# Moving one subtraction behind the sums that TensorE waits for, and reordering the rest of VectorE's and ScalarE's work around it

## The chip, the cores and the metric

One core of a Trainium2 chip. The metric is device time in microseconds (us) of the whole program, and lower is better. TensorE (PE in the profile) multiplies, VectorE (DVE) and ScalarE (ACT) do elementwise work, GpSimd (POOL) and SyncE (SP) start transfers. PEld is TensorE's loading of weights.

## The reference, cut to what matters

```python
m, k, n = 2048, 2048, 2048
x = np.matmul(a, b)
rms = np.sqrt(np.mean(x ** 2, axis=-1, keepdims=True) + eps)
return (gamma * x / rms).astype(np.float32)
```

## The kernel before: the parts that matter

The kernel cuts the 16 row blocks into groups of two and makes each group's product with seven block products in place of eight (the additions and subtractions of quarters of A and B that this needs are made beforehand, on VectorE). `a_sums(g, (5, 2, 1))` makes such sums of A's quarters, each 128x1024 of fp16. A product is eight matmuls over K into one PSUM bank.

Rows 0 to 3 are the head; for rows 2 and 3 the right half (called the pair) is made from seven products too. Its end overlaps with the start of the first regular group, G0, which holds blocks 4 (HB) and 5. This is the seam that the change edits:

```python
    p6 = new_bank()
    product(PAIR, 1, 6, p6)
    a_sums(G0, (5,))                          # needs block HB, which ScalarE copied
    nc.vector.tensor_tensor(out=x22, in0=pair[1], in1=x22, op=ALU.subtract)
    for g in range(2):
        turn(HB + 1, g)                       # TensorE transposes block HB + 1
        take_transposed(HB + 1, g, turned[HB + 1, g], nc.vector.tensor_copy)
    square_half(0, 1)
    square_half(1, 1)
    take_rms(0)                               # a tiny reduction, then a root on ScalarE
    a_sums(G0, (2, 1))                        # sum 2 needs block HB + 1
```

The group's half then runs product 5, 2, 1, 4, 3, 7, 6, with other work hooked in between (hook n stands after the n-th product):

```python
        at_hook(0)
        p2, p5 = new_bank(), new_bank()
        one, two = ((5, p5), (2, p2)) if first else ((2, p2), (5, p5))
        product(g, j, *one)
        nc.scalar.copy(out=c, in_=one[1])
        last_squares()
        at_hook(1)
        product(g, j, *two)                   # in the first half: the product of sum 2
        nc.vector.tensor_tensor(out=t, in0=two[1], in1=c, op=ALU.add)
        at_hook(2)
        p1 = new_bank()
        product(g, j, 1, p1)
        ...
```

## Time and profile before

| | kernel before |
|---|---|
| median of the first 3 executions | 221.98 us (221.81 to 222.76) |
| span of the profiled execution | 219.9 us |
| TensorE busy | 95% |
| start of sum 2's product / natural start | 69.32 / 68.69 us |

The page of the kernel before, parts 1 and 4 (busy time by engine; shares of the span in the chain of work that ended last):

```profile
PE 209.3 (95%) x1032; PEld 97.4 (44%) x1032; DVE 165.9 (75%) x326; ACT 127.0 (58%) x263; POOL 36.3 (16%) x75
...
PE 65%; DMA 23%; ACT 4%; POOL 2%; issue 1%; DVE 1%; ACTq 0%; POOLq 0%
```

TensorE is 95% busy but holds only 65% of the chain. The rest of the chain is loads (DMA) and a short stretch of ScalarE and VectorE ahead of 69.32; the prediction shows that stretch line by line. "Natural start" is used all through: the start of sum 5's product plus eight matmuls of 0.2157 us, which is when the next product could begin if nothing held it.

### The profile page before, as it was taken

To read this page: it belongs to the slowest core of one execution; us is meant where nothing else is said; L and a number is where in the kernel's file an instruction comes from. 1 tells how busy PE (TensorE), PEld (TensorE's weight loads), DVE (VectorE), ACT (ScalarE), POOL (GpSimd) and SP (SyncE) were. 2 spreads that over 40 slices of the span, in tenths; PEclk is the share of its full clock that TensorE was granted. 3 is DMA by queue.
4 is the path that set the end of the run, shared out by engine and by line. 5 is a ranking of instruction groups with operands and counts; after the bars stand their busy time and mean duration, and the time that the engine had idled before them with its cause. 6 is when DMAs were issued, how large, how long until landed. Compare 5 with 4: busy or idle time off the path is not lost.

```text
span 219.9 us, 3044 instructions
## 1 busy us (share of the span) xinstructions
PE 209.3 (95%) x1032; PEld 97.4 (44%) x1032; DVE 165.9 (75%) x326; ACT 127.0 (58%) x263; POOL 36.3 (16%) x75
## 2 busy tenths in 40 slices
PE   7799999999999999999999999999999999999970
PEld 3344544444454444444444444444444444444440
DVE  1128799999889999979795639946695659787781
ACT  2110002920599898688745997289747996334471
POOL 7544443343020002100200002000200000000040
PEclk9999999999999999999999999999999999999996
DMA  7999999999929895948799049965699249145045
GB/s 157 164 203 206 199 206 208 212 206 228 409 76 362 291 293 118 358 176 230 213 300 405 3 93 265 351 247 95 156 294 405 42 100 364 73 174 210 1 171 212
DMA packets 36864, 46.60 MB, mean 212 GB/s; under 512 B 22256, under 2 KB 26352, under 8 KB 35568
## 3 DMA queue, kind: packets, MB, share of 16 engines
q0 software_dynamic: 10608, 23.86, 44.1%
q1 hardware_dynamic: 25824, 22.02, 33.5%
q10 hardware_dynamic: 416, 0.52, 0.7%
q8 instruction: 8, 0.13, 0.2%
q14 instruction: 8, 0.07, 0.1%
HBM read 34.60 MB, written 16.78 MB: 234 GB/s over the span
## 4 chain that ended last, share of the span: by engine, by line
PE 65%; DMA 23%; ACT 4%; POOL 2%; issue 1%; DVE 1%; ACTq 0%; POOLq 0%
PE acc L285 64%; DMA b<-in_b_dram 14%; DMA early<-in_a_dram 5%; DMA a<-in_a_dram 4%; ACT sq L219 2%; POOL b L102 1%; ACT at_even L192 1%; PE acc L790 1%; POOL early L106 1%; DVE s L260 1%; DVE at_even L192 0%; ACT x L729 0%; DVE x L551 0%; ACT norm L222 0%; ACT x L531 0%
## 5 line engine op out<-in xcount | busy, mean ns | idle before, releaser
L285 PE MATMUL acc<-b,s 128*128 128x512 bf16 x408 | 93.3, 379 | 0.5 <-DVE s L260 0.5
L285 PEld LDWEIGHTS <-s 128*128 128x128 f16 (+1 forms) x512 | 49.9, 98 | 60.4 <-DVE s L260 1.0
L388 PE MATMUL acc<-b,head_at 128*128 128x512 bf16 x176 | 43.2, 379 | 1.2 <-DMA b<-in_b_dram 1.2
L303 ACT ACTIVATE sq<-x 128x512 bf16<-128x512 f32 x53 | 33.4, 630 | 6.9 <-DVE x L722 3.0
L370 DVE SCALAR_TENSOR_TENSOR x<-x,r,gamma_sb 128x1024 f32<-128x1024 f32 x28 | 34.8, 1282 | 0.7
L219 ACT ACTIVATE sq<-a 128x1024 bf16<-128x1024 f32 x24 | 25.3, 1053 | 2.1 <-DMA a<-in_a_dram 1.5
L388 PEld LDWEIGHTS <-head_at 128*128 128x128 bf16 x176 | 16.9, 98 | 20.6 <-issue 1.6
L242 ACT ACTIVATE head_at<-a,s 128x2048 f16<-128x2048 f32 x10 | 20.0, 1998 | 3.3 <-DVE s L229 3.3
L102 POOL DMA_DIRECT2D b<-in_b_dram x32 | 17.2, 540 | 20.8 <-DMA b<-in_b_dram 15.0
L430 ACT COPY x<-acc 128x512 f32<-128x512 f32 x5 | 2.9, 582 | 24.7 <-PE acc L388 24.7
L285 PEld LDWEIGHTS <-head_at 128*128 128x128 f16 (+1 forms) x112 | 10.9, 98 | 13.2
L285 PE MATMUL acc<-early,head_at 128*128 128x512 bf16 x64 | 14.5, 379 | 0.0
L285 PEld LDWEIGHTS <-at_even 128*128 128x128 f16 x96 | 9.4, 98 | 11.3
L285 PE MATMUL acc<-early,s 128*128 128x512 bf16 x56 | 14.2, 379 | 0.0
L260 DVE TENSOR_TENSOR s<-head_at 128x1024 f16<-128x1024 f16 (+5 forms) x22 | 13.4, 635 | 0.1
L609 DVE TENSOR_TENSOR x<-x,x 128x512 f32<-128x512 f32 x9 | 6.2, 692 | 8.8 <-ACT x L607 8.3
L127 POOL COPY pace<-x 128x1 f32<-128x1 f32 x4 | 1.7, 413 | 66.7 <-DVE x L618 65.6
L591 ACT COPY x<-acc 128x512 f32<-128x512 f32 x9 | 5.2, 573 | 11.5 <-PE acc L285 11.5
L173 DVE COPY head_at<-tbank 128x1024 bf16<-128x1024 bf16 x7 | 4.8, 692 | 8.7 <-PE tbank L168 8.5
L285 PE MATMUL acc<-t_left,s 128*128 128x512 bf16 x48 | 11.3, 379 | 0.0
L774 POOL TENSOR_SCALAR x<-x,r 128x512 f32<-128x512 f32 x1 | 2.7, 2652 | 51.2 <-DVE r L346 51.2
L276 DVE TENSOR_TENSOR b<-b 128x1024 bf16<-128x1024 bf16 x16 | 10.8, 684 | 0.2
(113 smaller groups left out, 237.5 us busy)
## 6 DMA issues: line engine op xcount, KB each, us to landing
out_dram<-x SPq DMA_DIRECT2D x29, 512.0 KB, 3.8
a<-in_a_dram POOLq DMA_DIRECT2D x10, 1024.0 KB, 8.7
b<-in_b_dram POOLq DMA_DIRECT2D x32, 256.0 KB, 10.0
a<-in_a_dram POOLq DMA_DIRECT2D x4, 512.0 KB, 9.8
early<-in_a_dram POOLq DMA_DIRECT2D x7, 256.0 KB, 10.2
gamma_sb<-in_gamma_dram POOLq DMA_DIRECT2D x2, 512.0 KB, 8.3
out_dram<-x SPq DMA_DIRECT2D x3, 256.0 KB, 2.6
out_dram<-a SPq DMA_DIRECT2D x1, 512.0 KB, 3.3
```

The lines of the kernel that those rows point to most:

```text
L102: nc.gpsimd.dma_start(out=raw[j][kp][:, t, :], in_=b[lo:lo + P, j * HALF:(j + 1) * HALF])
L173: nc.vector.tensor_copy(out=head_at[:, 2 * kp:2 * kp + 2, :, :], in_=view)
L219: nc.scalar.activation(out=junk, in_=a32[mb][:, h * HALF:(h + 1) * HALF], func=ACTF.Square, scale=2.0 ** -8, accum_out=n2[:, h:h + 1])
L242: nc.scalar.activation(out=a16[mb], in_=a32.pop(mb), func=ACTF.Copy, scale=factor.pop(mb))
L260: nc.vector.tensor_tensor(out=sum_of(g, s)[:, lo:hi, :], in0=x[:, lo:hi, :], in1=y[:, lo:hi, :], op=op)
L276: nc.vector.tensor_tensor(out=flat[:, 1:3, :], in0=flat[:, 1:3, :], in1=flat[:, 0::3, :], op=ALU.add)
L285: nc.tensor.matmul(bank, lhsT[:, kp, :], rhs, start=(start and kp == 0), stop=(kp == KP - 1), skip_group_check=not start)
L303: nc.scalar.activation(out=sq[:, 0:CH], in_=src, func=ACTF.Square, scale=inv_sqrt_n, accum_out=msq[mb][:, c:c + 1])
L370: nc.vector.scalar_tensor_tensor(out=x, in0=x, scalar=inverse_of[mb], in1=gamma_sb[:, h * HALF:(h + 1) * HALF], op0=ALU.mult, op1=ALU.mult)
L388: nc.tensor.matmul(bank, head_at[:, kt, r, :], head_rhs(c, kt), start=(kt == 0), stop=(kt == KT - 1))
L591: nc.scalar.copy(out=c, in_=one[1])
L609: nc.vector.tensor_tensor(out=t, in0=t, in1=x12, op=ALU.add)
```

## The change

The intent: the subtraction does not feed TensorE, so let it run behind A's sums, which do. Then the pair's rows 2 and 3 are finished ahead of the scaling of rows 0 and 1, and a square of row 2 goes to where ScalarE would wait. The diff, cut:

```diff
     a_sums(G0, (5,))
-    nc.vector.tensor_tensor(out=x22, in0=pair[1], in1=x22, op=ALU.subtract)
     for g in range(2):
         ...
     square_half(1, 1)
+    a_sums(G0, (2,))
     take_rms(0)
-    a_sums(G0, (2, 1))
+    a_sums(G0, (1,))
+
+    def pair_sub():
+        nc.vector.tensor_tensor(out=x22, in0=pair[1], in1=x22, op=ALU.subtract)
 ...
                 hook(1, take_rms, 1)
+                hook(2, pair_sub)
                 hook(2, row_factor, nxt)
-                hook(2, finish, 0, (0,))
                 hook(2, apply, nxt)
                 hook(2, row_norm, nxt + 1)
+                hook(2, pair_sums)
                 hook(2, a_sums, g, (7, 6))
-                hook(2, finish, 1, (1, 0))
+                hook(2, finish, 0, (0,))
+                hook(2, finish, 1, (1,))
                 hook(2, row_factor, nxt + 1)
-                hook(2, pair_sums)
                 hook(2, pair_ends)
+                hook(2, scale, 1, (0,))
                 hook(4, apply, nxt + 1)
-                hook(7, square_half, r2, 1)
+                hook(4, store, 1, (0,))
+                hook(7, late.insert, 0, (r2, None))
```

(`last_squares` now also takes an entry that stands for half a row.) Below, **part 1** is the subtraction and the order of sums 2 and 1, **part 2** the order of the rows, **part 3** the later square.

More of the change, by code (lines that the diff above doesn't have):

```diff
@@ L573, in last_squares @@
         while late:
-            square(*late.pop(0))
+            mb, x = late.pop(0)
+            if x is None:
+                square_half(mb, 1)
+            else:
+                square(mb, x)
     def group_half(g, j, hooks):
```

## The prediction

> **What bounds the kernel now.** I read the page first, then the chain of work that ended last, then TensorE's waits, then the timelines of the engines around the one place that stood out. The page gives PE 95% of a 219.9 us span, DVE 75%, ACT 58%, and puts PE at 65% of the chain. The chain, in order of time, shows where PE takes over for good (start, length, what):
>
> ```profile
> 66.05 0.69 DVE s L260
> 66.74 0.60 DVE x L551
> 67.34 0.27 DVE at_even L192
> 67.61 0.25 issue
> 67.86 0.68 DVE at_even L192
> 68.54 0.06 DVE tot L335
> 68.60 0.67 DVE s L260
> 69.27 0.05 issue
> 69.32 141.76 PE acc L285 x656
> ```
>
> The reader is to see two things. From 69.32 on there is one unbroken run of 656 matmuls, 141.76 us long: nothing that VectorE or ScalarE does after that is on the path, up to the last 9 us. And just before it the path runs through VectorE, item by item through the very stretch that the change edits: A's sum 5 (L260), the subtraction (L551), two copies of transposed A (L192), a tiny reduction (L335), A's sum 2 (L260). All the waits of the matmuls in the whole kernel are these (us in total, times, longest):
>
> ```profile
> PE acc L147 <- DVE pace L137: 1.4, 1, 1.4
> PE acc L388 <- DMA b<-in_b_dram: 1.2, 2, 0.7
> PE acc L285 <- DVE s L260: 0.5, 1, 0.5
> PE tbank L419 <- DVE head_at L173: 0.3, 1, 0.3
> ```
>
> Three belong to the start, which the change leaves alone. The third is the one that it can remove. TensorE's timeline gives its true size:
>
> ```profile
> 66.97 1.89 PE L285 MATMUL acc<-b,s 128*128 128x512 bf16 x8
> 69.32 1.90 PE L285 MATMUL acc<-b,s 128*128 128x512 bf16 x8 [0.46 <-DVE s L260]
> 71.06 1.89 PE L285 MATMUL acc<-t_left,s 128*128 128x512 bf16 x8
> ```
>
> Matmuls of one product start 0.216 us apart (8 of them are 1.73 us), so the product after the one at 66.97 could have started at 66.97 + 1.73 = 68.70. It started at 69.32: **0.62 us lost**, of which the view shows 0.46 as idle, because the last matmul's modelled 0.379 us overlaps the gap.
>
> **What the Trainium skill says.** "TensorE: Matmul & The Clock Gate", section "Wait — 56ns, not 53.3ns?", gives 215.7 ns from start to start for warm matmuls of 512 columns; the trace agrees (0.216 us, granted clock 1.00 here), so PE cannot go faster in this stage, only start sooner. "Perfetto Trace Analysis", section "Tensor Engine Instruction (MATMUL, LD_WEIGHTS)", says that a matmul's end is estimated and that ScalarE and VectorE are strict FIFO. The first is why I count starts; the second is why a subtraction that nothing needs yet can hold up a sum that PE needs: the trace shows VectorE's instructions in program order, 0.60 us from start to start. "PSUM — Partial Sum Buffer", Specifications, gives 8 banks; the kernel holds one for transposes and 7 for products. A delayed read of a bank can therefore stall a product, and that has to be checked below.
>
> **The change, part by part.** *1. The subtraction leaves the path.* Removed ahead of sum 2: one 128x512 subtraction that reads PSUM, 0.60 us from start to start (66.66 to 67.26), and the tiny reduction, 0.11 us (68.46 to 68.57), which hides in the wait of sum 2 for the second copy anyway. New times on VectorE: sum 5 from 66.05. The first copy waits for the transposes, which end at 66.68, so it starts at about 66.7 and the second at 67.3. The second ends at about 67.97 (0.68 each). Sum 2 reads what it wrote and started 0.03 after its end before (68.54 to 68.57): 68.0 to 68.7 with its 0.69. PE answered 0.06 after sum 2 ended (69.26 to 69.32): 68.75. PE's natural start is 68.70, so 0.05 us, at most 0.1, of the stall stays. **Gain: 0.62 − 0.05 to 0.10 = 0.52 to 0.57 us**, at the head of an unbroken PE run, so all of it goes through to the end unless a new stall takes it.
>
> *2. Sum 1 goes behind the reduction.* It runs from about 68.75 to 69.45; its product wants it at 68.75 + 1.73 = 70.48. Not on the path.
>
> *3. Work moved in the first half of the group.* This reorders VectorE without adding to it. The same operations stand there:
>
> ```profile
> 73.97 1.29 DVE L260 TENSOR_TENSOR s<-at_even 128x1024 f16<-128x1024 f16 x2
> 75.36 2.48 DVE L370 SCALAR_TENSOR_TENSOR x<-x,r,gamma_sb 128x1024 f32<-128x1024 f32 x2
> 79.78 0.68 DVE L565 TENSOR_TENSOR x<-acc,x 128x512 f32<-128x512 f32 x1
> 80.38 0.68 DVE L566 TENSOR_TENSOR x<-acc,x 128x512 f32<-128x512 f32 x1
> ```
>
> I replayed the new order with the old spacings (0.60 for a sum, 1.20 for a 128x1024 scaling, 0.75 for a row factor's four small ones, 1.3 for the two dependent pair sums). The add of the second product comes at 70.9; the subtraction at 71.5 to 72.2; the factor to 72.8; the pair sums to 74.1; sum 7 from 74.1 to 74.8, sum 6 to 75.4; three scalings, a factor and the pair ends then fall between 75.3 and 79.9, about a microsecond sooner than at 79.78 and 80.38; one scaling to 81.0. After that VectorE is where it was before, since the sum of the work is equal. PE wants sum 7 at 68.75 + 4 x 1.73 = 75.67: 0.8 us to spare. Sum 6 has 2 us.
>
> *4. Half a row of row 2 is squared later.* ScalarE's 1.06 us square moves from before the copy of the second half's first product (81.59, copy at 82.64) to after it, where ScalarE stood waiting 0.72 us for VectorE at 83.93. This frees banks and operands sooner on ScalarE, but PE waited for neither. Worth 0 to the end time.
>
> Sum: **−0.55 us**, so 221.98 − 0.55 = **221.4 us**.
>
> **The rivals.** *A: the held bank.* The subtraction is what frees the bank of the pair's product 1, and it now comes 4.8 us later (72.2 for 67.3). Were that the bank of the group's third product, wanted at 70.5, PE would stall 1.7 us and the time would be about 223.1. Against it: the bank numbers of the program before give the third product the bank that ScalarE frees at 66.5, and the pair's bank to the fourth new one, product 7. That one is wanted at 75.7, 3.4 us after the subtraction. With the assignment following the order of release, it should stay with product 7 or go to product 6.
>
> *B: the stores move behind a transpose.* Row 0's first half is now scaled by 76.6, after the queue of SyncE has begun a transpose:
>
> ```profile
> 74.67 3.18 SPq L195 DMA_TRANSPOSE head_at<-head_at  x1
> 77.91 1.05 SPq L376 DMA_DIRECT2D out_dram<-x  x2
> ```
>
> So that store is issued at about 77.9 in place of 74.1 and, with the page's 3.8 us to landing, its buffer is free near 81 to 82. ScalarE's copy of product 3 writes that buffer and ran at 80.23; row 1's half that the next half's first copy overwrites lands just after. ScalarE may thus wait 0.5 to 1.5 us. PE needs that first copy done before product 4 of the second half, at 68.75 + 9 x 1.73 = 84.3; I put its end at 83.0. A microsecond more delay than I reckon would start to cost; half a microsecond of the gain lost would give 221.9.
>
> *C: more than the stall is gained.* Excluded by the unbroken run: no other wait is there to take.
>
> *D: the gain is lost near the end,* where the last 9 us hang on stores and ScalarE. They follow PE's last matmuls, so they move with them.
>
> **Range and chances.** The gain is 0.5 to 0.6 us if neither A nor B bites, which I hold for about 85%. The three times before spread from 221.81 to 222.76, and a median of a few runs can be off by 0.2 to 0.4. That gives 221.0 to 222.1 for 8 in 10, with the upper part for B. Two per cent are 4.4 us, ten times the largest wait that the change can touch and more than twice rival A: within 2% 0.98, faster 0.01, slower 0.01.
>
> **What would show it.** Right: TensorE's waits list no entry, or one below 0.1 us, for the sums of A at L260; the gap from the product at 66.97 to the next is 1.73 to 1.85 us in place of 2.35; the unbroken run starts some 0.55 us sooner and no new wait stands in it; the pair ends run about a microsecond sooner; ScalarE's 0.72 us wait shrinks. Wrong: a PE wait on the subtraction (A), on ScalarE's copies in the second half (B), or sum 2 coming later than 68.8 because the copies of the transposed blocks wait longer for PE than I assume.

## The result, and the profile after

The changed kernel took 221.14 us (median of 6, 221.01 to 221.74); the kernel before, in the same rounds, 222.0 us. The ratio is 0.9962, interval 0.9941 to 0.9982: within 2%.

The page of the changed kernel, the same two parts:

```profile
PE 209.2 (95%) x1032; PEld 97.5 (44%) x1032; DVE 166.0 (76%) x326; ACT 126.9 (58%) x263; POOL 36.4 (17%) x75
...
PE 92%; DMA 3%; issue 1%; ACT 1%; POOL 1%; DVE 0%; ACTq 0%; POOLq 0%
```

No engine does less work. What differs in these two pages is the chain: TensorE's share is 65% before and 92% after. Most of that rise is not the change's: three later traces of the old order have 86 to 87%, and one of the new order (part 1 alone, again) has 68%, since a chain that meets a load follows the loads from there back. What the change took out of the chain is the short stretch of ScalarE and VectorE ahead of sum 2: it stands in the chain of all four traces of the old order, and in neither trace of the changed kernel. All waits of the changed kernel's matmuls (us in total, times, longest):

```profile
PE acc L147 <- DVE pace L137: 1.4, 1, 1.4
PE acc L388 <- DMA b<-in_b_dram: 1.0, 1, 1.0
PE tbank L419 <- DVE head_at L173: 0.4, 1, 0.4
```

The wait on L260 (A's sums) has left the list. That alone proves little: three later traces of the old order do not list it either, though TensorE lost 0.27 to 0.31 us there. The starts of the matmuls decide. TensorE's timeline of the changed kernel over the seam, and VectorE's:

```profile
66.88 3.73 PE L285 MATMUL acc<-b,s 128*128 128x512 bf16 x16
70.44 1.89 PE L285 MATMUL acc<-t_left,s 128*128 128x512 bf16 x8
```

```profile
65.77 0.69 DVE L260 TENSOR_TENSOR s<-at_even 128x1024 f16<-128x1024 f16 x1 [0.20 <-ACT at_even L192]
66.63 0.69 DVE L192 COPY at_even<-tbank 128x1024 f16<-128x1024 f16 x1 [0.17 <-PE tbank L185]
67.24 0.68 DVE L192 COPY at_even<-acc 128x1024 f16<-128x1024 f16 x1
67.96 0.69 DVE L260 TENSOR_TENSOR s<-at_even 128x1024 f16<-128x1024 f16 x1
```

The products of sums 5 and 2 are now merged into one entry of 16 matmuls. Sixteen unhindered ones take 3.62 us in this view and these took 3.73, so 0.1 us of stall is left. Sum 2 runs from 67.96 to 68.65, TensorE starts on it at 68.705, and its natural start was 68.606. VectorE now waits for TensorE here (0.17 us for the transposes) and not the other way round.

### The profile page after: what moved, and what is told of

Read it like the earlier page. It is cut to its first block, busy times and chain, and to the rows that moved or that the text cites. A ratio compares the mean times of both kernels' runs of the same rounds, so it can differ in the third digit from the quotient of the medians.

```text
span 219.3 us, 3043 instructions
## 1 busy us (share of the span) xinstructions
PE 209.2 (95%) x1032; PEld 97.5 (44%) x1032; DVE 166.0 (76%) x326; ACT 126.9 (58%) x263; POOL 36.4 (17%) x75
## 4 chain that ended last, share of the span: by engine, by line
PE 92%; DMA 3%; issue 1%; ACT 1%; POOL 1%; DVE 0%; ACTq 0%; POOLq 0%
PE acc L285 71%; PE acc L388 16%; DMA early<-in_a_dram 3%; PE tbank L419 2%; PE tbank L168 2%; PE acc L800 1%; POOL b L102 0%; PE tbank L185 0%; PE acc L185 0%; ACT x L739 0%; DVE head_at L173 0%; ACT sq L803 0%; ACT rms L352 0%; POOL t_left masks.py:199 0%; POOL t_left masks.py:197 0%
## 5 line engine op out<-in xcount | busy, mean ns | idle before, releaser
L219 ACT ACTIVATE sq<-a 128x1024 bf16<-128x1024 f32 x24 | 25.3, 1053 | 2.2 <-DMA a<-in_a_dram 1.6
L260 DVE TENSOR_TENSOR s<-head_at 128x1024 f16<-128x1024 f16 (+5 forms) x22 | 13.4, 636 | 0.1
```

The costliest lines, as they stand in the source:

```text
L219: nc.scalar.activation(out=junk, in_=a32[mb][:, h * HALF:(h + 1) * HALF], func=ACTF.Square, scale=2.0 ** -8, accum_out=n2[:, h:h + 1])
L260: nc.vector.tensor_tensor(out=sum_of(g, s)[:, lo:hi, :], in0=x[:, lo:hi, :], in1=y[:, lo:hi, :], op=op)
```

## The experiments

**How each trace was read.** In every trace the span is a sum of three: the start of sum 2's product, the time from there to the start of the last matmul, and a tail. The table has all of them, in us. "Copy" is the end of ScalarE's second copy of transposed block HB, which releases sum 5. The last column is the start of the product less that copy.

| kernel | copy | natural start | start | stall | to last matmul | tail | start − copy |
|---|---|---|---|---|---|---|---|
| before | 66.02 | 68.69 | 69.32 | 0.63 | 143.23 | 7.36 | 3.30 |
| before, again | 65.30 | 68.33 | 68.61 | 0.27 | 143.23 | 7.32 | 3.31 |
| without part 1 | 66.00 | 69.00 | 69.30 | 0.30 | 143.23 | 7.36 | 3.31 |
| without part 1, again | 65.73 | 68.73 | 69.04 | 0.31 | 143.24 | 7.34 | 3.31 |
| changed | 65.74 | 68.61 | 68.71 | 0.10 | 143.24 | 7.34 | 2.97 |
| changed, again | 68.61 | 71.65 | 71.75 | 0.10 | 143.23 | 7.29 | 3.14 |
| part 1 alone | 66.35 | 68.99 | 69.09 | 0.10 | 143.23 | 7.91 | 2.74 |
| part 1 alone, again | 66.46 | 69.09 | 69.19 | 0.10 | 143.23 | 7.34 | 2.74 |
| square undone | 65.56 | 68.48 | 68.58 | 0.10 | 143.23 | 7.29 | 3.02 |
| held bank | 65.77 | 68.72 | 68.82 | 0.10 | 144.84 | 7.31 | 3.05 |
| delay on the path | 65.54 | 68.35 | 70.70 | 2.35 | 144.92 | 7.33 | 5.16 |
| delay beside | 65.72 | 68.75 | 68.85 | 0.10 | 143.48 | 7.32 | 3.13 |
| sum 2 in halves | 66.96 | 69.59 | 69.59 | 0.00 | 143.46 | 7.30 | 2.64 |

Two laws stand in it. In the old order the product starts 3.3 us after the copy, in four traces of four; TensorE was ready before that in all four. In the new order it starts 0.10 us after TensorE's natural start, in seven traces of seven that kept the seam as it is. Apart from the three kernels that put in work or a held bank, and a wait of 0.23 us in the last trace, everything else is the 143.23 us that none of the reorderings touched, and starts and tails that differ from execution to execution.

### The changed kernel again

> The changed kernel once more, beside the others on the same chip. Theory (the gain is the PE stall ahead of A's sum 2, 0.53 us by the starts of the matmuls in the two traces): 0.5 us under the kernel before, ratio 0.9976. Rival (the moved work and the square help too, so that the 0.86 us between the medians is real): 0.8 to 0.9 us under it, ratio 0.996. In the profile: 1.82 us from the start of the last product but one of A's sum 5 to the product of sum 2, as in the first trace.

221.3 us, the kernel before 222.14 in the same rounds, ratio 0.9977 (0.9937 to 1.0016). The profile happened to catch a poor start: TensorE waited 2.7 us for a load of B in the head, where it had waited 1.0 us in the first trace. For the next 3.4 us TensorE was then granted half of its full clock, and everything came 3 us later (a line of the view of busy time in stretches, explained at the delay on the path below; 0.50 is the granted clock):

```profile
8.82:12.23 3.41, 3.39 (x9) 1.15 (x9) 0.00 (x0) 0.00 (x0) 1.84 (x5) 0.50 1.23 203
```

The stall ahead of sum 2 was 0.10 us all the same. The times do not part theory from rival: the ratio is the theory's, but the medians lie 0.84 us apart, as the rival said. The structure of the trace fits the theory.

### Part 1 alone, twice

```diff
 (the kernel before)
+    the subtraction removed from the seam, sum 2 ahead of take_rms(0), sum 1 behind it
+                hook(2, pair_sub)
                 hook(2, row_factor, nxt)
                 hook(2, finish, 0, (0,))
```

> The kernel before with only the subtraction moved to the start of the later stretch, and sum 2 ahead of the tiny reduction; rows 0 to 3 in the old order, the square in its old place. Theory: the whole gain, 0.5 us under the kernel before and within 0.2 us of the changed kernel; PE's wait for sum 2 is 0.1 us or gone, and no new PE wait later. Rival (the other parts carry a share): 0.2 us or more slower than the changed kernel.

222.03 us, the kernel before 222.14, ratio 0.9996 (0.9969 to 1.0023): by the times a miss for the theory. By the trace it has the short stall (0.10) and no new wait, but a late start and the one long tail of 7.91. So it ran again:

> Part 1 alone, a second time, since its times (222.03) came out like those of the kernel before although its trace has the short gap. Theory (part 1 is the cause; its first trace had late loads by chance, product at 69.10, and a long tail, 7.91): a product near 68.7 to 69.1, 0.1 us of PE stall, and a median 0.3 to 0.6 us under the kernel before. Rival (parts 2 and 3 carry the gain in time, by the tail or by the start): 222.0 again, with a tail of 7.9 again.

221.18 us, the kernel before 221.43 in these rounds, ratio 0.999 (0.997 to 1.001). The stall was 0.10 again and the tail 7.34. The rival's repeated long tail did not come: the 0.57 us by which the first trace's tail was longer belonged to that execution. A gain of 0.25 us between medians is what the seam can explain, but it is less than the 0.3 to 0.6 us expected, and the interval of the ratio includes none. Part 1 also moves the tiny reduction behind sum 2. The two steps were not run apart, but the traces part them: sum 2 starts 0.03 us after the end of the second copy in the old order (68.54, 68.57) and in the changed kernel (67.92, 67.96), so the reduction held nothing up and the subtraction did.

### The rest without part 1, twice

```diff
 (the changed kernel)
     a_sums(G0, (5,))
+    nc.vector.tensor_tensor(out=x22, in0=pair[1], in1=x22, op=ALU.subtract)
 ...
-    a_sums(G0, (2,))
     take_rms(0)
-    a_sums(G0, (1,))
+    a_sums(G0, (2, 1))
 ...
-                hook(2, pair_sub)
```

> The changed kernel with the subtraction put back ahead of the transposed copies and sums 2 and 1 together behind the reduction; the new order of rows and the later square kept. Theory: no gain, within 0.2 us of the kernel before; the gap ahead of the product of sum 2 is 2.35 us again, 0.62 us of it lost. Rival: 0.2 to 0.4 us faster than the kernel before.

221.55 us, the kernel before 222.14, ratio 0.9988 (0.9947 to 1.0028). The stall came out at 0.30, not the 0.62 that was expected: the order of work is the old one, but TensorE was later in this execution (natural start 69.00), while the product started at 69.30 as before. That is what gave the law of the 3.3 us. The median lies 0.59 us under that of the kernel before: by the times alone the rival won this round, though the interval of the ratio includes 1. So it ran again:

> The rest without part 1, a second time, since its median (221.55) lay between the two kernels. Theory: product again at landing plus 10.2 us, a stall of 0.2 to 0.6 us, time like the kernel before within 0.3 us. Rival: 221.5 again, 0.5 us under the kernel before, with a shorter tail or an earlier start that the trace shows.

221.39 us, the kernel before 221.43, ratio 0.9997 (0.9978 to 1.0017); start − copy 3.31 again, 143.24 and 7.34. Parts 2 and 3 alone show no gain in either trace, nor in these times.

### The kernel before, again

> The kernel before, submitted as if it were a change, for a second trace of it. Reading of the six traces so far: the span is the start of sum 2's product, plus 143.23 us of unbroken matmuls (the same in all six), plus a tail of 7.3 us (once 7.9). In the old order the product starts 10.20 us after the load of the first A block has landed on its last DMA engine (59.12 and 69.32; 59.10 and 69.30), or when PE is through, whichever is later. Theory: that sum holds again (product at landing plus 10.2, 143.23, tail 7.3 or 7.9), and times like those of the kernel before. Rival: something in the 143 us differs in its slower executions, so that the trace shows another figure there.

221.45 us against 221.43, ratio 1.001 (0.9974 to 1.0046). The same kernel against itself gives an interval of 0.7%, so these rounds cannot tell a few tenths of a us; the traces can. The chain of work of this trace (start, length, what):

```profile
65.33 0.69 DVE s L260
66.02 0.60 DVE x L551
...
67.89 0.67 DVE s L260
...
68.61 141.76 PE acc L285 x656
```

It is the chain that the prediction shows, 0.7 us sooner. TensorE was sooner by only 0.36 (68.33 for 68.69), so the stall shrank from 0.63 to 0.27. ScalarE's timeline shows where the other 0.36 went, in the first trace of the kernel before and then in this one:

```profile
57.18 0.59 ACT L520 COPY x<-acc 128x512 f32<-128x512 f32 x1 [11.64 <-PE acc L285]
57.93 1.06 ACT L219 ACTIVATE sq<-a 128x1024 bf16<-128x1024 f32 x1 [0.16 <-DMA a<-in_a_dram]
```

```profile
56.82 0.59 ACT L520 COPY x<-acc 128x512 f32<-128x512 f32 x1 [11.64 <-PE acc L285]
57.30 1.06 ACT L219 ACTIVATE sq<-a 128x1024 bf16<-128x1024 f32 x1
```

In both, TensorE releases ScalarE's copy at L520, and TensorE's natural start comes 11.51 us after that copy's start. In this trace the squares of block HB (L219) followed without a wait, and ScalarE's second copy of transposed HB ended 8.48 us after the start of L520. In the first trace both squares waited for the two halves of block HB's load, which landed at 57.84 and 59.12, and it was 8.84 us. **So some 0.27 us of the stall belongs to the order of the work, as both chains start at the same work of TensorE; the other 0.36 us of the first trace is the lateness of block HB's load.** In the two traces without part 1 it is 8.51 and 8.52 us, and the stall 0.30 and 0.31. The law that was expected, 10.20 us from the landing to the product, gave 10.27 here, since the load held nothing up.

### The square in its old place

```diff
 (the changed kernel)
-                hook(7, late.insert, 0, (r2, None))
+                hook(7, square_half, r2, 1)
```

> The changed kernel with the square of row 2 back in its old place, ahead of the second half's first copy. Theory (the square's place is worth nothing): within 0.2 us of the changed kernel, 221.1 to 221.4; ScalarE waits some 0.7 us again before the late squares; no new PE wait. Rival (the square carries a share): 221.5 or more.

221.6 us, the kernel before 221.43, ratio 1.0012 (0.9982 to 1.0042). In the trace no new wait of TensorE, 143.23 us, a tail of 7.29, and the profiled execution is among the fastest of all (220.88 us). So nothing in the trace charges the square. The median of the times is on the rival's side (221.5 or more), but they spread from 220.88 to 223.07, and the interval allows up to 0.2% faster and 0.4% slower than the kernel before. ScalarE's timeline, the changed kernel first, then this one:

```profile
81.55 0.57 ACT L598 COPY x<-acc 128x512 f32<-128x512 f32 x1
82.02 1.06 ACT L310 ACTIVATE sq<-x 128x1024 bf16<-128x1024 f32 x1
...
83.89 0.63 ACT L303 ACTIVATE sq<-x 128x512 bf16<-128x512 f32 x1 [0.72 <-DVE x L620]
```

```profile
81.55 1.06 ACT L310 ACTIVATE sq<-x 128x1024 bf16<-128x1024 f32 x1
...
82.60 0.57 ACT L598 COPY x<-acc 128x512 f32<-128x512 f32 x1
83.76 0.63 ACT L303 ACTIVATE sq<-x 128x512 bf16<-128x512 f32 x1 [0.59 <-DVE x L620]
```

The copy and the square have changed places; the wait after them is not filled, since the same two pieces of work stand ahead of the same add of VectorE. Only the copy comes sooner, and TensorE did not need it.

### The held bank, forced

```diff
 (the changed kernel)
-        p1 = new_bank()
+        p1 = pair[1] if first else new_bank()
```

> The changed kernel, but the group's third product (A's sum 1) is made to take the very bank that the late subtraction reads. This is rival A of the prediction, forced. Theory (a late read of a bank costs only where the next product in that bank is already waiting): PE waits at that product until the subtraction ends at about 72.0, 1.6 us after its natural start at 70.44, and all of it goes through to the end: 1.6 us slower than the changed kernel, 1.1 slower than the kernel before. Rival (slack further on swallows part of such a stall): under 1.2 us slower than the changed kernel.

222.75 us, the kernel before 222.14 in the same rounds, ratio 1.0043 (1.0005 to 1.0081); 1.45 us over the changed kernel. The first line of TensorE's waits in this trace, and then a line of its timeline:

```profile
PE acc L285 <- DVE x L561: 1.4, 1, 1.4
```

```profile
72.17 1.89 PE L285 MATMUL acc<-t_left,s 128*128 128x512 bf16 x8 [1.45 <-DVE x L561]
```

L561 is the late subtraction. The run to the last matmul grew from 143.23 to 144.84: 1.61 us, with nothing given back. So rival A of the prediction is a real mechanism of the right size; the changed kernel escapes it only because that bank goes to the group's last product, which starts long after the subtraction. (That assignment was read from the built program; the changed kernel's traces show only that no matmul waits on L561.)

### A delay on the path, and one beside it

```diff
 (the changed kernel; gamma_sb is in place by then, and the result is not used)
+    def idle_work(n):
+        for _ in range(n):
+            nc.vector.reduce_sum(out=idle, in_=gamma_sb[:, HALF:], axis=mybir.AxisListType.X)
 (on the path)
+    idle_work(2)
     a_sums(G0, (2,))
 (beside it)
                 hook(2, scale, 1, (0,))
+                hook(2, idle_work, 1)
```

> The changed kernel with two useless VectorE reductions of 128x1024 put ahead of sum 2; each should take about 1.2 us from start to start, like a 128x1024 scaling. Theory (work ahead of sum 2 is on the path, and nothing later swallows it): the product of sum 2 starts at its natural time plus 0.1 plus 2.4, the run of matmuls after it stays 143.23 us, tail 7.3: 2.4 us slower than the changed kernel. Rival (a delay here is partly absorbed later): a run shorter than 143.23, under 2 us slower.

224.19 us (223.31 to 225.39), the kernel before 221.61, ratio 1.0098 (1.0046 to 1.0149). The two reductions took 2.4 us from start to start; the stall was 2.35 where 2.5 was expected. But the run after it did not stay at 143.23: it grew to 144.92. The view of busy time in stretches (us, PE, PEld, DVE, ACT, POOL busy with counts, granted clock, DMA share, GB/s) shows why:

```profile
66.00:68.00 2.00, 2.00 (x22) 1.29 (x19) 1.89 (x4) 1.97 (x4) 0.00 (x0) 1.00 0.85 344
71.00:74.60 3.60, 3.60 (x11) 1.25 (x10) 2.30 (x5) 3.00 (x7) 0.00 (x0) 0.53 0.67 275
74.60:80.00 5.40, 5.40 (x27) 2.45 (x26) 5.22 (x13) 4.16 (x5) 0.00 (x0) 1.00 0.22 54
```

After the stall TensorE was granted 0.53 of its clock for 3.6 us: matmuls started 0.427 us apart from 71.16 to 74.15, against 0.216 before and after. So this wait was paid a second time, by 144.92 − 143.23 = 1.69 us. Neither theory nor rival had that; the delay was not absorbed, it was amplified. The held bank's 1.6 us stall was followed by no such stretch. The times of this kernel lie 2.1 us apart, so not every execution need have had it. The mean granted clocks fit that, 0.989 and 0.983 at 224.72 and 225.39 us and 0.996 at 223.66 and 223.31, but only the first was traced. The poor start of the changed kernel's second trace shows the same pair, a wait of 2.7 us and then 3.4 us at half the clock.

> The changed kernel with one such reduction, 1.2 us of VectorE, put behind the last scaling of the moved stretch. Theory (that stretch is beside the path with a known slack): the add of the second half's second product then ends 1.2 us later, at about 86.25 on the clock of the first changed trace. Product 3 accumulates into the bank that it reads and starts at 85.98, so PE waits there 0.2 to 0.4 us, and nowhere else: 0.2 to 0.4 us slower, not 1.2. Rival (VectorE is as good as the bound here): 1.2 us slower.

221.41 us, the kernel before 221.61, ratio 0.9996 (0.9949 to 1.0044). VectorE's timeline and TensorE's:

```profile
81.08 1.21 DVE L142 TENSOR_REDUCE idle<-gamma_sb 128x1 f32<-128x1024 f32 x1
...
85.65 0.68 DVE L608 TENSOR_TENSOR x<-acc,x 128x512 f32<-128x512 f32 x1
```

```profile
84.40 3.87 PE L291 MATMUL acc<-early,at_even 128*128 128x512 bf16 x16
```

The reduction pushed the add at L608 to 85.65 to 86.33, and TensorE's 16 matmuls of products 4 and 3 took 3.87 us in place of 3.62: 0.25 us of wait in the place that was named, and 143.48 in the table. Of 1.2 us added to VectorE, 0.25 reached the end. VectorE at 76% is close to the bound in this stretch, with some 0.9 us to spare, but it is not the bound.

### Sum 2 in two halves

```diff
 (the changed kernel)
-    a_sums(G0, (2,))
+    a_sums(G0, (2,), 0, KP // 2)
+    a_sums(G0, (2,), KP // 2, KP)
```

> The changed kernel with sum 2 made in two halves, so that the first four matmuls of its product can start on the first. Theory (the 0.10 us that PE still waits in every trace of the new order is the sum's own 0.69 us): the first half takes 0.4 us, PE starts at its natural time, stall 0.0 to 0.02, so 0.1 us under the changed kernel, too little for the times to show; the second half costs VectorE some 0.15 us beside the path. Rival (the matmuls wait for the whole tile all the same): a stall of 0.2 us.

221.13 us, the kernel before 221.61, ratio 0.9966 (0.9933 to 0.9999). The stall is gone to the last hundredth: TensorE's timeline has the clean 3.62 us for the 16 matmuls.

```profile
67.87 3.62 PE L285 MATMUL acc<-b,s 128*128 128x512 bf16 x16
```

This is the best seam of all, worth 0.10 us over the changed kernel by the trace, and in the fastest of its executions the lowest time seen (220.59 us). The times can't show 0.10 us. Its trace had one thing more, a 0.23 us wait at 109.3 before the second half's product 4 of the next group. There ScalarE's copy ended at 109.49, 2.6 us later than in the first changed trace while TensorE was later by 0.9: the load of block 8 landed at 93.45 and not 90.81. That is a second seam where loads and TensorE race; none of the other traces of the reorderings lost time there. Whether the halves had a part in it was not tried.

## Why the prediction was right or wrong

The time, 221.14 us, lies in the stated range, and within 2% was right. The range has room for any gain from nothing to 0.98 us, so that alone says little of the 0.55 us reckoned. Step by step:

- **The bound.** Right: 143.23 us of matmuls from sum 2 on, the same to 0.01 us in all nine traces whose change did not stall them further on. All that the change could touch was the start of that run.
- **Part 1, the size of the gain.** The mechanism was right and the first pair of traces fits to the hundredth (stall 0.63 to 0.10, so 0.53, predicted 0.52 to 0.57; the residue of 0.10 was the upper end of what was given). What was mis-sized is the term "0.62 us lost", taken from one execution as if it were the kernel's. Four traces of the old order show 0.63, 0.27, 0.30 and 0.31: some 0.27 of it is the order of the work, and the other 0.36 was a late load of block HB in that execution. The first trace of the kernel before is the one from which the gain was worked out, so its fit is no second measurement. An estimate over all 13 traces, from the two laws of the table (old start = copy + 3.305, new start = natural start + 0.10; the old one less the new one in each), gives 0.16 to 0.57 us, mean 0.34: the least where the load was in time, the most where it was so late that TensorE's natural start was late too (11.65 to 12.08 us after L520). The 0.86 us between the first medians is more than the seam can give. The kernel before alone moved from 222.14 to 221.43, on two chips, so the remainder is most likely scatter of starts and tails; the six ratios of kernels with the new seam and no added wait average 0.9984, or 0.36 us, which agrees with the estimate, but they run from 0.9962 to 1.0012.
- **Sum 1 and the moved work.** Right: no wait of TensorE in that stretch. The subtraction ended at 72.00 (predicted 72.2), sum 7 at 74.74 (74.8), the pair ends at 79.82 (79.9).
- **The square.** Worth nothing in any trace, as predicted. Wrong was the sign named for it: ScalarE's 0.72 us wait was said to shrink, and it stayed at 0.72. Work that only changes places in front of a wait does not fill it.
- **Rival A.** Right both ways: the changed kernel does not meet it, and forced it cost 1.61 us where 1.7 was reckoned.
- **Rival B.** The stores did move behind the transpose. They landed at 80.19 and 81.40, not near 81 to 82 and later, and ScalarE's two copies started at 80.32 and 81.55, just behind them. So no wait arose. The transpose came sooner than reckoned: SyncE was through with it at 76.65, and in the trace before at 77.85.
- **Rival C** ("more than the stall is gained: excluded") looked doubtful after the first 0.86 us and after part 1's first times. The second round of each removed the doubt, by the trace more than by the times.
- **Rival D.** Right: the tail moved with the matmuls, 7.36 us before and 7.34 after.
- **A slip.** Two per cent are 4.4 us, seven times the 0.62 us of the prediction and not ten; nothing hangs on it.

## What to carry to other kernels

On an engine that takes its work in order, look at what stands ahead of the operand that the bounding engine waits for next, and put behind it everything that feeds nothing yet; check first which buffer the postponed work keeps and who wants that buffer. A stall between two chains of which one waits for a load can differ from execution to execution: take several traces, write the start as the later of two sums, and part what the order costs from what the load adds, before you price it. When a change is worth a few tenths of a per cent, an account of the span in parts (start, run, tail) decides what timing rounds can't.

## What the Trainium skill lacked or had wrong

- "TensorE: Matmul & The Clock Gate", section "HAM oscillation — how this bites in real kernels", gives as the rule no idle gaps over about 3.4 us. In one trace here a stall of 2.35 us (2.57 from one start to the next) was followed by 3.6 us at a granted clock of 0.53, at a cost of 1.69 us; in another a wait of 2.7 us was followed by 3.4 us at 0.50. A stall of 1.61 us was not. A gap clearly under the rule's figure can already be charged twice.
- "Perfetto Trace Analysis" says that a matmul's end is estimated, and the runs agree. It does not say what that does to idle time: the loss of 0.63 us ahead of sum 2 stood in the waits as 0.5, and losses of 0.27 to 0.31 us, and the 0.10 that remains, did not appear among the matmuls' waits at all. Spacing of starts showed them.
- None of the pages that I read gives how far the parts of one load lie apart when they land. In one trace (the rest without part 1) the second half of block HB was complete at 59.10 us, while 12 of its 16 parts had landed by 57.85 and the first by 57.06. Nor do they give how far the same load moves between executions: it was complete at 58.34, 58.83, 58.85, 59.10, 59.12, 59.46 and 59.56 us in seven traces.
